# A decoder block with its residual turned by VectorE and small DMAs instead of TensorE, and its last outputs reordered

## The chip, the cores and the metric

One core of a Trainium2 chip runs the whole program. The metric is device time in microseconds (us) of one execution; the time before is 696.47 us, the median of three runs (696.46 to 696.84). The profile is one further execution of the same program, taken by the hardware profiler.

The engines are named as in the profile: PE is TensorE, PEld its weight load, DVE is VectorE, ACT is ScalarE, POOL is GpSimd, SP only issues DMAs. A "q" behind a name (SPq, ACTq) is that engine's queue issuing a DMA.

## The reference

One layer of a decoder on 512 positions with a model width of 1024, in float32. The parts in order:

```
h   = rms_norm(x, mix_norm)
z   = h @ w_in                       # u, v, c_q, c_kv, k_rope, gate_A, gate_B
y_a = gelu(u) * (tril(W_s) @ layer_norm(gelu(v)) + b)      # per chunk of 128 positions
y_b = latent attention of c_q, c_kv, k_rope                # 8 heads, causal
x   = x + (sigmoid(gate_A) * y_a + sigmoid(gate_B) * y_b) @ w_out
h   = rms_norm(x, ffn_norm)
up  = causal conv of width 3 of (h @ w_up)                 # 1024 -> 2 * 2816
x   = x + (silu(up[:2816]) * up[2816:]) @ w_down           # 2816 -> 1024
out = rms_norm(x, final_norm)
```

## The kernel before

Almost all work is matrix products. Each product of two float32 matrices is done as three TensorE products of operands split into a high part (rounded by an ACT copy to the type that PE takes) and a low part (the rest, a DVE subtraction): `mm3`, lines 79 to 82. A weight tile of 128 x 1024 is loaded into `wr` (three buffers), split into `wh` and `wl` (three buffers each, `wsplit`, lines 65 to 73), and used.

Activations stand transposed, with channels on partitions and the 512 positions along the row, in all parts but the last. The stages in time are: the small projections (`pS`, from 5 us on), v, the attention and gates, the product with w_out (`pout`), which leaves the residual `x1[j]`, eight tiles of 128 channels x 512 positions, then the up-projection (`pup`, 336 to 581 us) and the down-projection (`m`, 581 to 687 us).

The up-projection is a loop over n = 0 to 21 (line 653). Each n does two chunks of 24 matmuls (`up`, lines 621 to 628), the convolution (`conv`), the gate, and now and then `a_sides`, which prepares sums for the down-projection. The output must have positions on partitions, so the residual is turned on the way: for n = 4 to 11, `x1_turn` (lines 645 to 650) makes four PE transposes of 128 x 128 into a PSUM bank and an ACT copy of the bank back over the tile `x1t`. A turned row of 512 channels then lies in four pieces of 128 (512 bytes each).

The down-projection is computed in the manner of Strassen with seven products, in the order m1, m5, m6, m4, m3, m7, m2 (line 689). Each has 11 blocks of k in six steps (two blocks each, one in the last) for two output tiles (m = 0 and 1). The right-hand weights are sums that are formed by accumulating DMAs on POOL's queue into six tiles `R[g]` (`fill`, lines 604 to 608); the first fill and the one before m3 are plain loads on SP's queue. m2 reads its weights through `wr`. `a_split` (line 694) splits the left sides into tiles of tags h0 to h5, `w_split` (line 711) the weights two steps ahead. `post` (lines 751 to 775) adds the products to the residual; after the last product that touches an output tile, `done` adds it and has ACT square and sum it, and `finish` (lines 736 to 747) forms the inverse root on POOL, scales one half on DVE and the other on ACT, and stores both, one on SP's and one on ACT's queue. In m2 the last three steps are run for output tile 0 first and then for tile 1, so that tile 0 is finished while PE works on tile 1.

The order on each engine comes from a planner: it walks through the program with modelled costs and gives each engine the ready instruction that stands first in the program, so an instruction can run long before its place in the loop. A tile of a tag waits until the tile that held its buffer is no longer read.

The names that the change touches: `x1t` and `vA2` (lines 178 and 560, they share buffers by the tags d0 and d1), `x1_turn`, `fill`, `a_split`, `w_split`, `res`, `done`, `finish`, the loops of lines 653 and 796, and at the start the order of loads (lines 186 to 202) and the sum of squares `acc` (lines 211 to 222).

## Time and profile before

| what | value |
|---|---|
| median of three runs | 696.47 us (696.46 to 696.84) |
| the profiled execution | 697.01 us, of which the span from first to last instruction is 695.3 us |
| PE busy | 684.6 us (98% of the span), 3183 matmuls |
| DVE, ACT, POOL busy | 522.6, 353.9, 36.0 us |
| granted clock of PE, mean | 0.996 |
| HBM read, written | 76.02 MB, 2.10 MB |
| the last matmul begins | 686.15 us |

A row of the timeline has the start in us, the duration in us, engine, line, operation, the tile written, the tile read, and in brackets the idle time of that engine before it with what ended it. Matmuls overlap on PE, so the step from one start to the next says what one costs; the duration is longer than that.

### The profile page before, as it was taken

The numbers are of one execution on the slowest core, as the hardware profiler recorded it, in microseconds if no ns is written. First come the engines' busy times: TensorE is split into PE (matmuls) and PEld (weight loads), VectorE is DVE, ScalarE is ACT, GpSimd is POOL, SyncE is SP. The second block draws the span as 40 slices with busy tenths as digits, with TensorE's granted clock in tenths as the row PEclk, the third lists the DMA queues.
The fourth block names the chain that finished last, engine by engine and source line by source line (L and its number), as shares of the span: only waits on it lengthen the run. The fifth ranks groups of instructions, "written<-read, shape, count | busy, mean of one in ns | idle before, by whom it ended". The sixth has DMA issues, their size and how long they took to land.

```text
span 695.3 us, 8489 instructions
## 1 busy us (share of the span) xinstructions
PE 684.6 (98%) x3183; PEld 569.4 (82%) x3183; DVE 522.6 (75%) x859; ACT 353.9 (51%) x519; POOL 36.0 (5%) x42
## 2 busy tenths in 40 slices
PE   9999999999999999999999999999999999999994
PEld 6888888888888888888888888888888888888883
DVE  7966699877768678855577868778677789579884
ACT  6465556775765552343354344444344335565672
POOL 0000110000000000000100000000000002330201
PEclk9999999999999999999999999999999999999998
DMA  8424522131120112353542222223322236997824
GB/s 269 153 78 139 186 84 83 61 115 31 61 88 34 62 61 91 109 177 107 180 170 90 92 91 90 92 90 99 114 91 91 91 91 118 197 187 202 159 76 122
DMA packets 28026, 78.67 MB, mean 113 GB/s; under 512 B 3024, under 2 KB 7632, under 8 KB 27984
## 3 DMA queue, kind: packets, MB, share of 16 engines
q1 hardware_dynamic: 21408, 62.92, 27.4%
q0 software_dynamic: 3456, 11.54, 9.3%
q10 hardware_dynamic: 3120, 3.67, 1.7%
q8 instruction: 25, 0.41, 0.2%
q14 instruction: 17, 0.14, 0.1%
HBM read 76.02 MB, written 2.10 MB: 112 GB/s over the span
## 4 chain that ended last, share of the span: by engine, by line
PE 96%; DVE 1%; issue 1%; POOL 0%; ACT 0%; POOLq 0%
PE pup L80 12%; PE pup L82 12%; PE pup L81 11%; PE m L82 4%; PE m L81 4%; PE m L80 4%; PE pout L81 2%; PE pv L80 2%; PE pout L80 2%; PE pza L81 2%; PE pza L80 2%; PE pzb L80 2%; PE pzb L82 2%; PE pzu L81 2%; PE pzb L81 2%; PE pv L82 2%
## 5 line engine op out<-in xcount | busy, mean ns | idle before, releaser
L70 ACT CAST wh_u<-wr_u 128x1024 fp32r<-128x1024 f32 x44 | 46.3, 1051 | 84.4 <-issue 49.6
L71 DVE TENSOR_TENSOR wl_u<-wr_u,wh_u 128x1024 fp32r<-128x1024 f32 x44 | 53.9, 1224 | 9.9 <-ACT wh_u L70 9.6
L635 DVE TENSOR_TENSOR z<-pup,r 128x512 f32<-128x512 f32 x44 | 30.3, 690 | 40.3 <-PE pup L82 40.3
L82 PE MATMUL m<-wh_m,al_m 128*128 128x512 f32 x132 | 51.5, 390 | 0.6 <-DVE al_m L77 0.6
L80 PE MATMUL m<-wh_m,ah_m 128*128 128x512 f32 x132 | 51.4, 389 | 0.0
L81 PE MATMUL m<-wl_m,ah_m 128*128 128x512 f32 x132 | 51.4, 389 | 0.0
L70 ACT CAST wh_g<-wr_g 128x1024 fp32r<-128x1024 f32 x24 | 25.2, 1049 | 49.4 <-issue 30.6
L71 DVE TENSOR_TENSOR wl_m<-r,wh_m 128x1024 fp32r<-128x1024 f32 (+1 forms) x36 | 40.7, 1131 | 6.3 <-ACT wh_m L70 6.3
L70 ACT CAST wh_m<-r 128x1024 fp32r<-128x1024 f32 (+1 forms) x36 | 35.3, 980 | 19.6 <-PE m L82 19.1
L637 ACT ACTIVATE y<-z,part 128x512 f32<-128x512 f32 x44 | 35.7, 814 | 2.6 <-DVE z L635 2.4
L663 ACT ACTIVATE y<-y 128x512 f32<-128x512 f32 x22 | 13.9, 633 | 45.0 <-DVE y L641 45.0
L606 POOL DMA_DIRECT2D r<-in_w_d_dram x24 | 21.4, 890 | 287.0 <-DVE wl_m L71 270.7
L71 DVE TENSOR_TENSOR wl_g<-wr_g,wh_g 128x1024 fp32r<-128x1024 f32 x24 | 29.4, 1223 | 7.2 <-ACT wh_g L70 7.1
L641 DVE SCALAR_TENSOR_TENSOR y<-z,part,y 128x512 f32<-128x512 f32 x44 | 33.0, 751 | 1.4
L639 DVE SCALAR_TENSOR_TENSOR y<-z,part,y 128x512 f32<-128x512 f32 x44 | 32.8, 747 | 0.7 <-ACT y L637 0.7
L82 PEld LDWEIGHTS m<-wh_m,al_m 128*128 128x128 f32 x132 | 24.8, 188 | 6.1 <-DVE al_m L77 1.0
L81 PEld LDWEIGHTS m<-wl_m,ah_m 128*128 128x128 f32 x132 | 24.8, 188 | 5.2
L80 PEld LDWEIGHTS m<-wh_m,ah_m 128*128 128x128 f32 x132 | 24.8, 188 | 5.2
L81 PE MATMUL pout<-mL,wh_o 128*128 128x512 f32 x64 | 25.3, 395 | 0.0
L80 PE MATMUL pout<-mH,wh_o 128*128 128x512 f32 x64 | 25.0, 394 | 0.0
L82 PE MATMUL pout<-mH,wl_o 128*128 128x512 f32 x64 | 24.9, 389 | 0.0
L77 DVE TENSOR_TENSOR al_m<-aT,ah_m 128x1024 fp32r<-128x1024 f32 (+1 forms) x12 | 13.6, 1134 | 11.9 <-ACT ah_m L76 11.9
(565 smaller groups left out, 2004.0 us busy)
## 6 DMA issues: line engine op xcount, KB each, us to landing
wr_u<-in_w_u_dram SPq DMA_DIRECT2D x44, 512.0 KB, 3.3
wr_g<-in_w_g_dram SPq DMA_DIRECT2D x24, 512.0 KB, 3.4
r<-in_w_d_dram POOLq DMA_DIRECT2D x20, 512.0 KB, 7.2
r<-in_w_d_dram SPq DMA_DIRECT2D x10, 512.0 KB, 6.1
x<-in_xT_dram SPq DMA_DIRECT2D x16, 256.0 KB, 4.5
wr_v<-in_w_v_dram SPq DMA_DIRECT2D x8, 512.0 KB, 4.1
wr_o<-in_w_o_dram SPq DMA_DIRECT2D x8, 512.0 KB, 3.2
wr_m<-in_w_d_dram SPq DMA_DIRECT2D x5, 512.0 KB, 3.5
```

The lines of the kernel that those rows point to most:

```text
L70: A.copy(th[:, lo:hi], raw[:, lo:hi])
L71: V.tensor_tensor(out=tl[:, lo:hi], in0=raw[:, lo:hi], in1=th[:, lo:hi].bitcast(F32), op=ALU.subtract)
L77: V.tensor_tensor(out=tl, in0=src, in1=th.bitcast(F32), op=ALU.subtract)
L80: T.matmul(o, lhsT=wh, rhs=xh, start=start, stop=False)
L81: T.matmul(o, lhsT=wh, rhs=xl, start=False, stop=False)
L82: T.matmul(o, lhsT=wl, rhs=xh, start=False, stop=stop)
L606: G.dma_start(R[g], q[:, cols(g)], accum_op=ALU.add)
L635: V.tensor_tensor(out=z[:, 2:], in0=pz, in1=r2, op=ALU.mult)
L637: A.activation(out=y, in_=z[:, 2:], func=AF.Identity, scale=part[:, w + 2:w + 3], bias=part[:, PCB + f:PCB + f + 1])
L639: V.scalar_tensor_tensor(out=y, in0=z[:, 1:S + 1], scalar=part[:, w + 1:w + 2], in1=y, op0=ALU.mult, op1=ALU.add)
L641: V.scalar_tensor_tensor(out=y, in0=z[:, 0:S], scalar=part[:, w:w + 1], in1=y, op0=ALU.mult, op1=ALU.add)
L663: A.activation(out=yg, in_=yg, func=AF.Silu)
```

## The change

The residual is turned in two steps. `squares` has DVE transpose each `x1[j]` in blocks of 32 x 32 into a tile `xq` (eight instructions, n = 0 to 3). `x1_turn` then moves the blocks to their places in a new tile `xt` with DMAs on POOL's queue, each of 32 partitions x 4 x 32 elements (rows of 128 bytes): eight in each of n = 4 to 19, 128 in all. `xt` takes the buffer of `x1t`, which is now one tile, and `xq` the buffers of `R[0]` to `R[3]`. The first fill of `R` moves to n = 16 to 21 in the order 4, 5, 0, 1, 2, 3, and all fills go to POOL's queue.

In the down-projection the left side's last block of m2 gets tiles of its own and is split earlier (step 4 in place of 8); two of m2's six weight steps are split into buffers of `R`; `post` of a product is written three steps later in the program; m2's last four steps, not three, are run by output tile. `done` sums both halves' squares into the same cell and prepares all but one operation of the root; `finish` writes its result to a tile `o`, whose rows of 512 elements are stored as 2 KB each; tiles 0 and 2 share an `o` buffer, and so do tiles 1 and 3.

At the start, the first quarter of the first weights is loaded by ACT's queue ahead of everything else there, and the additions of squares come after the loop over j.

The diff, cut to what is spoken of:

```diff
+    ws0 = wp.tile([P, 1024], F32, tag="wr", name="wr_s0")
+    A.dma_start(ws0[:, :256], w_s[0, :, :256])
...
-    vA2 = [hp.tile([P, 2 * D], F32, tag=f"d{t}", name=f"vA{t}") for t in range(2)]
-    vA = [vA2[t // 2][:, (t % 2) * D:(t % 2 + 1) * D] for t in range(NT)]
+    vA4 = hp.tile([P, NT, D], F32, tag="d", name="vA")
+    vA = [vA4[:, t] for t in range(NT)]
...
-                    raws.append(wp.tile([P, 1024], F32, tag="wr", name="wr_s0"))
-                    for c in (slice(0, 256), slice(256, S)):
-                        SY.dma_start(raws[0][:, c], w_s[0, :, c])
+                    SY.dma_start(ws0[:, 256:S], w_s[0, :, 256:S])
...
-            sq = acc if j == 0 else st.tile([P, S], F32, tag="sq", name=f"sq{j}")
+            sq = acc if j == 0 else st.tile([P, S], F32, tag="sq", name=f"sq{j}", bufs=KC - 1)
+            sqx.append(sq)
...
-            if j:
-                V.tensor_tensor(out=acc, in0=acc, in1=sq, op=ALU.add)
+        for sq in sqx[1:]:
+            V.tensor_tensor(out=acc, in0=acc, in1=sq, op=ALU.add)
...
-        x1t = [hp.tile([P, NT, NT, P], F32, tag=f"d{t}", name=f"x1_{t}") for t in range(2)]
-        x1 = [x1t[j // NT][:, j % NT].rearrange("p t c -> p (t c)") for j in range(KC)]
+        x1t = hp.tile([P, KC, S], F32, tag="d", name="x1")
+        x1 = [x1t[:, j] for j in range(KC)]
...
-    R = [fp.tile([P, (hi - lo) * S], F32, name=f"r1_{lo}") for lo, hi in steps]
+    xq = [fp.tile([P, D], F32, tag=f"rr{q}", name=f"xq{q}") for q in range(KC // 2)]
+    R = [None] * NS
...
     def fill(q, g, add=True):
+        if R[g] is None:
+            R[g] = fp.tile([P, D], F32, tag=f"rr{g}", name=f"r1_{g}")
         if add:
-            G.dma_start(R[g], q[:, cols(g)], accum_op=ALU.add)
+            G.dma_start(R[g][:, :q[:, cols(g)].shape[1]], q[:, cols(g)], accum_op=ALU.add)
         else:
-            SY.dma_start(R[g], q[:, cols(g)])
+            G.dma_start(R[g][:, :q[:, cols(g)].shape[1]], q[:, cols(g)])
...
-    def x1_turn(t, hf):
-
-        pt = bank(f"pt{t}{hf}")
-        for q in range(NT):
-            T.transpose(pt[:, q * P:(q + 1) * P], x1t[hf][:, q, t, :], ident)
-        A.copy(x1t[hf][:, :, t, :], pt.rearrange("p (q c) -> p q c", q=NT))
+    def squares(j):
+        V.transpose(out=xq[j // 2][:, (j % 2) * S:(j % 2 + 1) * S], in_=x1[j])
+
+    xt = []
+
+    def x1_turn(j, rows):
+
+        if not xt:
+            xt.append(hp.tile([P, NT, D], F32, tag="d", name="xt"))
+        q = xq[j // 2][:, (j % 2) * S:(j % 2 + 1) * S].rearrange("p (t c f) -> p t c f", t=NT, c=NT)
+        for a in rows:
+            for c in range(NT):
+                G.dma_start(xt[0][32 * c:32 * c + 32, :, j * P + 32 * a:j * P + 32 * a + 32],
+                            q[32 * a:32 * a + 32, :, c])
...
-            if 4 <= n < 12:
-                x1_turn((n - 4) // 2, n % 2)
-            if 12 <= n < 12 + NS:
-                fill(B11, n - 12, False)
+            if n < 4:
+                squares(2 * n)
+                squares(2 * n + 1)
+            elif n < 20:
+                x1_turn((n - 4) // 2, (0, 1) if n % 2 == 0 else (2, 3))
+            if n >= NF - NS:
+                fill(B11, (n - NF + NS + 4) % NS, False)
...
-        ah = hp.tile([P, D], F32R, tag=f"h{b}", name=f"ah_{n}{lo}")
-        al = hp.tile([P, D], F32R, tag=f"h{3 + b}", name=f"al_{n}{lo}")
+        own = n == "m2" and b == 2
+        ah = hp.tile([P, D], F32R, tag=f"h{6 if own else b}", name=f"ah_{n}{lo}")
+        al = hp.tile([P, D], F32R, tag=f"h{7 if own else 3 + b}", name=f"al_{n}{lo}")
...
-        ws_[n, g] = wsplit(raw, f"{n}{g}", 0, w)
+        tiles = None
+        if n == "m2" and g in (2, 3):
+            tiles = tuple(fp.tile([P, D], F32R, tag=f"rr{2 * (g - 2) + k}", name=f"m2{g}{k}") for k in range(2))
+        ws_[n, g] = wsplit(raw, f"{n}{g}", 0, w, tiles)
...
-        return x1t[f][:, :, t, :]
-
-    def b3(t):
-        return t.rearrange("p (q c) -> p q c", q=NT)
+        return xt[0][:, t, f * S:(f + 1) * S]
...
+    def done(t, f, p_, op=ALU.add, last=False):
+        V.tensor_tensor(out=res(t, f), in0=res(t, f), in1=p_, op=op)
         j_ = dp.tile([P, S], F32, tag="j", name=f"j{t}{f}", bufs=2)
-        A.activation(out=b3(j_), in_=res(t, f), func=AF.Square, accum_out=ms[:, t, f:f + 1])
+        A.activation(out=j_, in_=res(t, f), func=AF.Square, accum_out=ms[:, t, 0:1])
+        if not last:
+            V.tensor_scalar(out=ms[:, t, 1:2], in0=ms[:, t, 0:1], scalar1=1.0 / D, scalar2=EPS,
+                            op0=ALU.mult, op1=ALU.add)
         if f:
-            V.tensor_tensor(out=res(t, f), in0=res(t, f), in1=b3(gfb[:, S:]), op=ALU.mult)
+            V.tensor_tensor(out=res(t, f), in0=res(t, f), in1=gfb[:, S:], op=ALU.mult)
...
-        V.tensor_scalar(out=ms[:, t, 2:3], in0=ms[:, t, 0:1], scalar1=ms[:, t, 1:2], scalar2=1.0 / D,
-                        op0=ALU.add, op1=ALU.mult)
-        V.tensor_scalar(out=ms[:, t, 2:3], in0=ms[:, t, 2:3], scalar1=EPS, scalar2=None, op0=ALU.add)
+        V.tensor_scalar(out=ms[:, t, 2:3], in0=ms[:, t, 0:1], scalar1=1.0 / D, scalar2=ms[:, t, 1:2],
+                        op0=ALU.mult, op1=ALU.add)
         G.tensor_tensor(out=ms[:, t, 3:4], in0=ms[:, t, 2:3], in1=mhalf[:, 0:1], op=ALU.pow)
         r_ = ms[:, t, 3:4]
-        V.scalar_tensor_tensor(out=res(t, 0), in0=res(t, 0), scalar=r_, in1=b3(gfb[:, :S]),
+        o = fp.tile([P, D], F32, tag=f"rr{(4, 5, 4, 5)[t]}", name=f"o{t}")
+        V.scalar_tensor_tensor(out=o[:, :S], in0=res(t, 0), scalar=r_, in1=gfb[:, :S],
                                op0=ALU.mult, op1=ALU.mult)
-        A.mul(res(t, 1), res(t, 1), r_)
-        SY.dma_start(out[t, :, :S], res(t, 0))
-        A.dma_start(out[t, :, S:], res(t, 1))
+        A.mul(o[:, S:], res(t, 1), r_)
+        SY.dma_start(out[t, :, :S], o[:, :S])
+        A.dma_start(out[t, :, S:], o[:, S:])
...
-            turn_.setdefault(b if i == 1 else NS * (i - 1) + (4, 6, 8)[b], []).append((n, b))
+            turn_.setdefault(b if i == 1 else NS * (i - 1) + (4, 6, 4 if n == "m2" else 8)[b], []).append((n, b))
...
+    late = {}
     for i, (n, g) in enumerate(seq):
         if i + 2 < len(seq):
             w_split(*seq[i + 2])
+        if i in late:
+            post(*late[i])
         for x in turn_.get(i, ()):
             a_split(*x)
         if g == 0:
             acc_ = [bank(f"{n}_{m}") for m in range(2)]
-        if n != order[-1] or g < NS - 3:
+        if n != order[-1] or g < NS - 4:
             steps_of(n, g, (0, 1))
             if g == NS - 1:
-                post(n, acc_)
+
+                late[i + 3] = (n, acc_)
 
     for m in range(2):
-        for g in range(NS - 3, NS):
+        for g in range(NS - 4, NS):
```

## Rows read from the trace of the kernel before

**Rows 1.** the page: busy time of each engine, with share of the span and instructions.
```profile
PE 684.6 (98%) x3183; PEld 569.4 (82%) x3183; DVE 522.6 (75%) x859; ACT 353.9 (51%) x519; POOL 36.0 (5%) x42
```

**Rows 2.** the page: the chain that ended last, share of the span by engine.
```profile
PE 96%; DVE 1%; issue 1%; POOL 0%; ACT 0%; POOLq 0%
```

**Rows 3.** windows: stretch, length, busy us of each engine (instructions), granted clock, DMA share, GB/s.
```profile
336.00:460.00 124.00, 124.00 (x563) 102.67 (x563) 88.38 (x134) 53.65 (x70) 1.84 (x1) 1.00 0.35 117
```

**Rows 4.** chain in order of time (start, us, what): first and last of eight.
```profile
392.08 0.44 PE pt L649 x4
...
471.64 0.44 PE pt L649 x4
```

**Rows 5.** PE in order of time: first products of two pup tiles, two chunks apart.
```profile
553.54 0.39 PE L80 MATMUL pup<-h0f,wh_u 128*128 128x512 f32 x1
...
564.42 0.39 PE L80 MATMUL pup<-h0f,wh_u 128*128 128x512 f32 x1
```

**Rows 6.** all engines in order of time, PE's wait in the last product.
```profile
680.97 0.39 PE L82 MATMUL m<-wh_m,al_m 128*128 128x512 f32 x1
...
681.94 0.50 PE L82 MATMUL m<-wh_m,al_m 128*128 128x512 f32 x1 [0.58 <-DVE al_m L77]
```

**Rows 7.** all engines in order of time, from the last outputs to the last store.
```profile
683.86 0.69 DVE L730 TENSOR_TENSOR x<-x,m 128x512 f32<-128x512 f32 x1 [1.37 <-PE m L82]
...
686.15 0.39 PE L82 MATMUL m<-wh_m,al_m 128*128 128x512 f32 x1
686.39 0.75 DVE L743 SCALAR_TENSOR_TENSOR x<-x,ms,gfb 128x512 f32<-128x512 f32 x1 [0.66 <-POOL ms L741]
687.06 0.68 DVE L730 TENSOR_TENSOR x<-x,m 128x512 f32<-128x512 f32 x1
...
688.53 0.21 DVE L738 TENSOR_SCALAR ms<-ms 128x1 f32<-128x1 f32 x1 [0.79 <-ACT j L732]
688.78 0.15 DVE L740 TENSOR_SCALAR ms<-ms 128x1 f32<-128x1 f32 x1
...
690.34 0.47 ACTq L747 DMA_DIRECT2D out_dram<-x  x1
```

**Rows 8.** DMA rate in 40 equal slices, 688 to 696 us, then 385 to 395.
```profile
GB/s 128 292 292 292 287 292 289 282 284 185 0 0 0 0 0 0 125 297 292 287 279 292 294 282 282 215 10 8 0 0 0 0 0 0 0 0 0 0 0 0
...
GB/s 360 442 393 311 33 0 0 0 0 0 0 0 66 0 0 0 0 0 0 0 0 164 164 49 377 377 442 426 99 0 0 0 0 0 0 0 0 0 0 0
```

**Rows 9.** the page: DMA issues: KB each, median us from issue to landing.
```profile
r<-in_w_d_dram POOLq DMA_DIRECT2D x20, 512.0 KB, 7.2
...
out_dram<-x ACTq DMA_DIRECT2D x4, 256.0 KB, 3.3
```

**Rows 10.** all engines in order of time, the first matmuls.
```profile
4.88 0.41 ACT L70 CAST wh_s<-wr_s 128x256 fp32r<-128x256 f32 x1 [0.49 <-DMA wr_s<-in_w_s_dram]
...
5.33 0.79 PE L80 MATMUL pS<-h0a,wh_s 128*128 128x512 f32 x1
...
5.92 0.63 PE L81 MATMUL pS<-h0a,wh_s 128*128 128x512 f32 x1
```

**Rows 11.** POOL in order of time: two DMA issues, one right behind the other.
```profile
614.12 0.88 POOL L606 DMA_DIRECT2D r<-in_w_d_dram  x1 [2.72 <-DVE wl_m L71]
615.41 0.88 POOL L606 DMA_DIRECT2D r<-in_w_d_dram  x1 [0.41 <-issue]
```

**Rows 12.** the page: DMA queues: packets, MB, share of 16 engines.
```profile
q0 software_dynamic: 3456, 11.54, 9.3%
q10 hardware_dynamic: 3120, 3.67, 1.7%
```

**Rows 13.** tile r: duration ns min/median/max, first and last start.
```profile
L606 POOL DMA_DIRECT2D r<-in_w_d_dram x24: 875/881/1063, 572.5 to 652.1; - x24
L608 SPq DMA_DIRECT2D r<-in_w_d_dram x12: 327/328/437, 339.7 to 636.1; - x12
```

**Rows 14.** ACT in order of time: the first read of r.
```profile
569.90 1.04 ACT L70 CAST wh_m<-r 128x1024 fp32r<-128x1024 f32 x1
```

More of the change, by code (lines that the diff above doesn't have):

```diff
@@ L177, in block_kernel @@
     ckL = mx.tile([P, S], F32R, name="ckL")
-    vA2 = [hp.tile([P, 2 * D], F32, tag=f"d{t}", name=f"vA{t}") for t in range(2)]
-    vA = [vA2[t // 2][:, (t % 2) * D:(t % 2 + 1) * D] for t in range(NT)]
+    vA4 = hp.tile([P, NT, D], F32, tag="d", name="vA")
+    vA = [vA4[:, t] for t in range(NT)]
     with tc.tile_pool(name="st", bufs=2) as st:
-        raws = []
+        raws = [ws0]
         xr = []
@@ L204, in block_kernel @@
         sw = [None] * 4
+        sqx = []
         for j in range(KC):
@@ L719, in res @@
     def res(t, f):
-        return x1t[f][:, :, t, :]
-    def b3(t):
-        return t.rearrange("p (q c) -> p q c", q=NT)
+        return xt[0][:, t, f * S:(f + 1) * S]
     def plus(t, f, t_):
-        V.tensor_tensor(out=res(t, f), in0=res(t, f), in1=b3(t_), op=ALU.add)
-    def done(t, f, p_, op=ALU.add):
-        V.tensor_tensor(out=res(t, f), in0=res(t, f), in1=b3(p_), op=op)
+        V.tensor_tensor(out=res(t, f), in0=res(t, f), in1=t_, op=ALU.add)
+    def done(t, f, p_, op=ALU.add, last=False):
+        V.tensor_tensor(out=res(t, f), in0=res(t, f), in1=p_, op=op)
@@ L769, in post @@
                 done(2 + m, 0, b[m])
-                done(2 + m, 1, b[m], ALU.subtract)
+                done(2 + m, 1, b[m], ALU.subtract, True)
                 finish(2 + m)
@@ L773, in post @@
                 with tc.high_priority():
-                    done(m, 0, b[m])
+                    done(m, 0, b[m], last=True)
                     finish(m)
```

## The prediction, made before the changed kernel was run

> **What bounds the kernel now.** I read the page's busy times first: PE is busy for 684.6 of 695.3 us, DVE for 522.6, POOL for 36.0 [rows 1]. The chain of waits then says that this work is also the path: 96% of the chain is PE [rows 2]. So time is won by taking matmul work from PE, by filling the few holes in PE's row, and by shortening what comes before the first and after the last matmul. In the stretch of the up-projection PE is busy for all 124.00 of 124 us, DVE for 88.38 and POOL for 1.84, and the DMA engines for 0.35 of the time [rows 3]; DVE has 36 us free there and POOL nearly everything. The only hole in PE's row of the down-projection is in the last product [rows 6], and after the last matmul, which begins at 686.15, come some 9 us of VectorE, ScalarE and store work [rows 7].
>
> **The sum is made against the profiled execution**, 697.01 us with a span of 695.3 (1.7 us lie outside the span). That execution is 0.54 us above the median of 696.47, so the result is carried over by taking the savings from the median.
>
> **PE transposes out.** The eight groups of four transposes begin at 392.08 to 471.64, one per n: (471.64 - 392.08) / 7 = 11.37 us per n with a group [rows 4]. Two chunks without one take 564.42 - 553.54 = 10.88 us (48 matmuls at 0.227) [rows 5]. A group thus costs PE 0.49 us and the eight 3.9 us. The chain books 0.44 for a group, which gives 3.5 as the lower end; 4.0 is the upper. PE has no holes here, so all of it is on the path. Their eight ACT copies go too; ACT is not on the path.
>
> **What takes their place.** Eight DVE transposes of 128 x 512: the trace has none. The nearest row is a 128x512 addition, 0.69 us [rows 7], so 5.5 us in all; at four times that, 22 us, they would still fit the 36 us that DVE has free before 460 [rows 3]. I cost them at nothing for PE, since weights are split two chunks (10.9 us) ahead; without that cover a transpose would cost its 0.7 us once or twice. Their place in the program is n = 0 to 3, but the planner runs what is ready: the first fill of `R`, written in n = 12, was issued at 339.7 [rows 13]. I expect the transposes in DVE's gaps before about 350.
>
> 128 DMAs on POOL's queue: each has 32 x 4 rows of 128 bytes, 128 pieces, as many as a fill has (3456 packets for 24 fills are 144 each, 128 and 16 that carry no data) [rows 12]. A fill costs POOL 0.88 us, 1.06 at most [rows 13], and two that stand right behind each other begin 1.29 us apart [rows 11]. I take 1.29: 128 x 1.29 = 165 us, from 350 to 515 us. Behind them POOL has the six first fills, 8 us to issue and 7.2 us to land [rows 9], so `R` is there at about 531; ACT first reads it at 569.90 [rows 14]. On POOL nothing else waits in that stretch. The bounds are 0.88 us (113 us in all) and a DMA that begins only when the one before has landed, at least the 3.3 us of a store (422 us); the limit is where the fills come late, (569.9 - 350 - 15) / 128 = 1.6 us. On the DMA engines, a packet of POOL's queue took 9.3% x 16 x 695.3 / 3456 = 0.30 us (4 KB, accumulating), one of ACT's queue 1.7% x 16 x 695.3 / 3120 = 0.06 us (1.2 KB on average) [rows 12]. 128 x 144 packets at 0.06 are 69 us of all 16 engines, which with the 0.35 in use fit 165 us. I take 0.06, since size decides more than the queue; at 0.30 they would be 346 us, and that belongs to the slower case below. The fills that move from SP's to POOL's queue cost SP nothing and POOL 0.9 us each. So: 3.9 won, 0 given back.
>
> **The hole in m2.** Two matmuls stand 681.94 - 680.97 = 0.97 us apart in place of 0.23, ended by DVE's `al_m` [rows 6], the block of the left side that now has its own tiles and an earlier place: 0.74 us won. Bounds 0 (another wait appears at the same place) and 0.8. The weights of m2 get two steps' worth of extra buffers, so the splits need not wait for PE; I see no stall that would be late next.
>
> **After the last matmul.** It ends at 686.54. For tile 1 the addition begins at 687.06, because DVE still has the scaling of tile 0 (686.39) in hand; for tile 0 it began as soon as PE was done [rows 7]. With four steps by tile instead of three, tile 0 is done 6 matmuls = 1.36 us earlier and that queueing of 0.5 us goes. Of the two small operations 0.25 us apart (688.53, 688.78) one remains: 0.25 won. Together 0.75; bounds 0.25 and 0.8. The scaled results go to `o` at the same cost.
>
> **The store.** The last two stores move 0.52 MB at about 292 GB/s in rows of 512 bytes, 1.8 us; loads with 4 KB rows reach 442 [rows 8], which would take 1.2. In rows of 2 KB I take 400 GB/s: 1.3 us, 0.5 won. Bounds 0 (the rate is that of writing) and 1.2 (issue and landing shorten too).
>
> **The start.** PE's first real matmul (5.33) waits for ACT's cast, which had waited 0.49 us for the first weights, and the second comes 0.59 us later [rows 10]; matmuls that wait for nothing stand 0.23 apart [rows 5]. With the load on ACT's queue at once, the cast no longer waits: 0.3 won. The warm-up matmuls stand in front of it on PE and keep it from being much more. Bounds 0 and 0.6. The additions of squares are moved behind the loop; they are the same seven, and their reader on PE stands behind the whole stage: 0.
>
> **Sum:** 3.9 + 0.74 + 0.75 + 0.5 + 0.3 = 6.2 us, 690.8 against the profiled execution and 690.3 against the median. The lower ends give 3.5 + 0 + 0.25 + 0 + 0 = 3.75, thus 692.7; the upper 7.4, thus 689.1.
>
> **The rivals.**
> *POOL or the small packets are too slow (slower).* If each small DMA holds POOL for over 1.6 us, the first fills land after ACT wants them and PE stops in front of m1, with nothing later to catch up. At 2.1 us (between 1.29 and 3.3): 350 + 128 x 2.1 + 15 = 634, then 2.3 us for cast and subtraction, so m1 starts at 636 and not at 580.75 less the 3.9 won: +59 us, about 750. At 0.30 us per packet the same happens through the DMA engines. Against it: POOL's 0.88 us doesn't wait for landing, since 1.29 us between two issues is far below 7.2 [rows 9, 11]. What would decide is whether 128 in a row keep that pace, which no row shows.
> The Trainium skill (DMA: Bandwidth & Descriptors, "Anatomy of one DMA") speaks against the change in this way: a DMA from POOL's queue has a fixed cost of about 2.0 us whatever its size. If that cost were paid one after the other, 128 x 2.0 = 256 us would put this rival's time near 737; if it overlaps, the forecast holds. The two issues 1.29 us apart bear out the overlap for two only.
>
> *The end is given back.* `post` of m7 is written three steps later (6 matmuls x 2 tiles per step, up to 6.8 us), and tile 0's result needs the `o` buffer that tile 2's store must have left (3.3 us to land) [rows 9]. In today's order that leaves some 2.7 us to spare; if the planner really moves tile 2's scaling by the whole 6.8 us, tile 0's scaling stands about 4 us in front of DVE's queue, and tile 1's addition behind it: +2.5 to 4 us on the forecast, about 693.5. For it: DVE works in order, and the last stage has it busy most of the time. Against it: the planner fills gaps, and with weights split earlier DVE has gaps before.
>
> *It changes nothing.* The PE time is real and PE's row has no holes, so this needs a loss that just cancels 4 to 6 us, such as DVE's transposes delaying the root of the second norm and then every chunk. Time 696.5.
>
> **How the numbers follow.** Forecast 0.67, the end given back 0.20, no change 0.05, too slow 0.08. A measurement of this kernel tells about 0.2% (1.4 us) from no change. Forecast and end given back are faster: 0.87; no change 0.05; slower 0.08. The forecast's own range is 689.1 to 692.7. To hold 8 in 10 it reaches to 694.3, through most of the second case, and down to 688.6; the too slow case is left out.
>
> **What would show each step.** Up-projection: no `pt` rows, chunks of 5.44 us throughout, PE busy for all of it. POOL: 128 DMA issues of about 0.9 us, 1.3 us apart, done near 515, and the first reading of `R` not ended by a DMA. Weight loads may land later than 3.3 us, harmless below 10. Last product: no matmul over 0.3 us behind its neighbour. End: addition within 0.05 us of the last matmul, one small DVE operation, store rate near 400 GB/s. The prediction is wrong if PE idles in front of m1, if DVE waits for a store ahead of writing `o`, or if POOL is still issuing small DMAs after 560.

## The result, and the profile after

The changed kernel takes 690.53 us (median of six runs, 690.25 to 692.8), the kernel before beside it 696.76 us (six, 696.46 to 697.14): a ratio of 0.9913, 95% interval 0.99 to 0.9927. The forecast was 690.3 us, its range 688.6 to 694.3. The profiled execution after is one of 690.42 us with a span of 688.6 us; all stretches below are of that one and of profiled executions of the other kernels.

The page of the kernel after, busy times and the chain:
```profile
PE 679.8 (99%) x3151; PEld 565.9 (82%) x3151; DVE 525.8 (76%) x867; ACT 350.0 (51%) x511; POOL 111.8 (16%) x182
...
PE 97%; issue 1%; DMA 0%; DVE 0%; ACT 0%; POOLq 0%; POOL 0%
```
PE has 32 instructions less than in [rows 1], the transposes, and is still the chain [rows 2]. POOL's 36.0 us became 111.8 us.

The window of the up-projection after, columns as in [rows 3]:
```profile
336.00:460.00 124.00, 124.00 (x552) 102.75 (x551) 95.16 (x146) 52.25 (x66) 75.27 (x135) 1.00 0.44 134
```
PE is as full as before, DVE has 6.8 us more and POOL 73 us more, and PE waits for neither.

The two new kinds of instruction, in the views of a line and of a tile (duration of one in ns, min/median/max, then first and last start in us; the landing is from issue to the data being there):
```profile
L653 DVE STREAM_TRANSPOSE xq<-x x8: 668/669/712, 339.3 to 346.3; 128x512 f32<-128x512 f32 x8
```
That is the line of the transposes; this is the tile that the DMAs write:
```profile
L664 POOL DMA_DIRECT2D xt<-xq x128: 551/551/617, 347.3 to 423.2; - x128
...
DMA to landing us min/median/max: 1.6/2.3/4.7
```
The 128 small DMAs begin (423.2 - 347.3) / 127 = 0.60 us apart, pauses included, half of the 1.29 that I took. Two of the six first fills were issued ahead of them, at 340.03; the other four come from 417.66 to 425.98, not behind 515:
```profile
408.92 8.69 POOL L664 DMA_DIRECT2D xt<-xq  x15 [0.15 <-issue]
417.66 0.58 POOL L615 DMA_DIRECT2D r<-in_w_d_dram  x1
418.24 1.72 POOL L664 DMA_DIRECT2D xt<-xq  x3
...
425.98 0.54 POOL L615 DMA_DIRECT2D r<-in_w_d_dram  x1 [1.00 <-DMA xt<-xq]
```

The end after, all engines in order of time; it answers to [rows 7]:
```profile
681.07 0.39 PE L82 MATMUL m<-wh_m,al_m 128*128 128x512 f32 x1
681.50 0.69 DVE L749 TENSOR_TENSOR xt<-xt,m 128x512 f32<-128x512 f32 x1 [1.66 <-PE m L82]
...
682.97 0.21 DVE L760 TENSOR_SCALAR ms<-ms 128x1 f32<-128x1 f32 x1 [0.79 <-ACT j L751]
...
683.85 0.75 DVE L765 SCALAR_TENSOR_TENSOR o<-xt,ms,gfb 128x512 f32<-128x512 f32 x1 [0.66 <-POOL ms L762]
684.60 0.37 ACTq L769 DMA_DIRECT2D out_dram<-o  x1
```
The addition begins 0.04 us after the last matmul's end (681.46), against 0.52 in [rows 7]. The last two stores, 684.6 to 688.6 us in 40 slices of 0.1 us (answers to [rows 8]; last columns of the issues: KB each, us to landing):
```profile
GB/s 0 0 0 0 0 0 0 0 143 348 369 451 348 410 348 369 369 471 369 369 369 369 144 0 0 0 0 0 0 0 0 0 0 0 0 0 0 0 0 0
...
out_dram<-o ACTq DMA_DIRECT2D x1, 256.0 KB, 2.8
```

Divided at four places that both kernels have, with a second profile of the kernel before (below, e10), the time went here (us):

| stretch | before | before again | after | won |
|---|---|---|---|---|
| start of the span to the first `pup` product | 336.05 | 335.40 | 335.74 | none shown |
| from there to the first product of m1 | 244.70 | 244.70 | 240.84 | 3.86 |
| to the start of the last product of m2 | 105.40 | 105.46 | 104.49 | 0.91 |
| to the issue of the last store | 4.19 | 4.18 | 3.53 | 0.66 |
| to the end of the span | 4.96 | 4.96 | 4.00 | 0.96 |

The last four rows of the kernel before repeat within 0.1 us; what is won in them adds up to 6.39 us, the medians differ by 6.23.

### The profile page after: what moved, and what is told of

It reads as the page before. It is cut to its first block, busy times and chain, and to the rows that moved or that the text cites. A ratio compares the mean times of both kernels' runs of the same rounds, so it can differ in the third digit from the quotient of the medians.

```text
span 688.6 us, 8556 instructions
## 1 busy us (share of the span) xinstructions
PE 679.8 (99%) x3151; PEld 565.9 (82%) x3151; DVE 525.8 (76%) x867; ACT 350.0 (51%) x511; POOL 111.8 (16%) x182
## 3 DMA queue, kind: packets, MB, share of 16 engines
q0 software_dynamic: 9152, 19.41, 13.6%
## 4 chain that ended last, share of the span: by engine, by line
PE 97%; issue 1%; DMA 0%; DVE 0%; ACT 0%; POOLq 0%; POOL 0%
PE pup L80 12%; PE pup L82 12%; PE pup L81 12%; PE m L82 5%; PE m L81 5%; PE m L80 5%; PE pout L81 2%; PE pv L80 2%; PE pout L80 2%; PE pza L81 2%; PE pza L80 2%; PE pzb L80 2%; PE pzb L82 2%; PE pzb L81 2%; PE pzu L81 2%; PE pv L82 2%
## 5 line engine op out<-in xcount | busy, mean ns | idle before, releaser
L664 POOL DMA_DIRECT2D xt<-xq x128 | 70.7, 553 | 9.0 <-DVE xq L653 3.8
L613 POOL DMA_DIRECT2D r<-in_w_d_dram x24 | 21.0, 873 | 188.9 <-DVE wl_m L71 167.5
L80 PE MATMUL m<-wh_m,ah_m 128*128 128x512 f32 x124 | 48.2, 389 | 0.0
L81 PE MATMUL m<-wl_m,ah_m 128*128 128x512 f32 x124 | 48.2, 389 | 0.0
L82 PE MATMUL m<-wh_m,al_m 128*128 128x512 f32 x124 | 48.2, 389 | 0.0
L615 POOL DMA_DIRECT2D r<-in_w_d_dram x12 | 6.9, 573 | 232.5 <-DVE acc L584 222.3
L80 PEld LDWEIGHTS m<-wh_m,ah_m 128*128 128x128 f32 x124 | 23.3, 188 | 4.9
L81 PEld LDWEIGHTS m<-wl_m,ah_m 128*128 128x128 f32 x124 | 23.3, 188 | 4.9
L82 PEld LDWEIGHTS m<-wh_m,al_m 128*128 128x128 f32 x124 | 23.3, 188 | 4.8
```

The costliest lines, as they stand in the source:

```text
L80: T.matmul(o, lhsT=wh, rhs=xh, start=start, stop=False)
L81: T.matmul(o, lhsT=wh, rhs=xl, start=False, stop=False)
L82: T.matmul(o, lhsT=wl, rhs=xh, start=False, stop=stop)
L613: G.dma_start(R[g][:, :q[:, cols(g)].shape[1]], q[:, cols(g)], accum_op=ALU.add)
L664: G.dma_start(xt[0][32 * c:32 * c + 32, :, j * P + 32 * a:j * P + 32 * a + 32], q[32 * a:32 * a + 32, :, c])
```

## The experiments

**e1: the transposes on PE again.** The edit, on the kernel after (the readers of the residual change only their views):
```
-            if n < 4:
-                squares(2 * n)
-                squares(2 * n + 1)
-            elif n < 20:
-                x1_turn((n - 4) // 2, (0, 1) if n % 2 == 0 else (2, 3))
+            if 4 <= n < 12:
+                x1_turn((n - 4) // 2, n % 2)
...
+            T.transpose(pt[:, q * P:(q + 1) * P], x1t[:, hf * NT + q, t * P:(t + 1) * P], ident)
+        A.copy(x1t[:, hf * NT:(hf + 1) * NT, t * P:(t + 1) * P], pt.rearrange("p (q c) -> p q c", q=NT))
```


> The kernel after, with one edit undone: the residual is turned by TensorE in place again (32 transposes of 128x128, ScalarE copies the banks back), no transposes on VectorE and no small DMAs on POOL; all other edits stay. Theory: PE sets the end, so its 32 transposes cost what they took in the kernel before: the first product of m1 starts at 576.6 + 3.9 = 580.4 us (580.0 to 580.6) and the median is 690.5 + 3.9 = 694.4 us (694.0 to 694.8). Rival: part of the gain came from ScalarE's and VectorE's load in the projection (the eight copies gone), and TensorE's transposes sat partly in its own small waits: then the first m1 product moves by less than 2.5 us and the median stays under 693.0 us.

Measured: 694.62 us median of five (694.27 to 696.12), 0.9971 of the kernel before (0.9957 to 0.9986). PE in order of time, the first product of m1:
```profile
580.92 0.39 PE L80 MATMUL m<-wh_m,a1h 128*128 128x512 f32 x1
```
That start is 0.3 us above the interval expected because this execution began late: its first `pup` product is at 336.22. Between the two lie 244.70 us, to the hundredth what the kernel before has. So the 3.86 us are the transposes' time on PE and nothing else, and with everything else of the change in place the kernel gives them back whole. The later stretches are those of the kernel after (104.50, 3.52 and 4.0 us), so the transposes are not what is won there.

**e2: stores in pieces of 512 bytes.**
```
-        V.scalar_tensor_tensor(out=o[:, :S], in0=res(t, 0), ...
+        ov = o.rearrange("p (q h c) -> p q h c", q=4, h=2)
...
+        V.scalar_tensor_tensor(out=ov[:, :, 0], in0=rv_[0], ...
...
-        A.dma_start(out[t, :, S:], o[:, S:])
+        A.dma_start(rv_[4], ov[:, :, 1])
```


> The kernel after, but the output tile is laid out with the two halves interleaved, so that each store takes four pieces of 512 bytes of a partition in place of one of 2 KB; bytes, queues and order are the same. Theory: the size of the rows made the last store shorter (4.96 to 4.00 us from its issue to the end of the span): here it is 4.9 us again (4.6 to 5.1), and the median is about 0.9 us up, 691.4 us. Rival: the last stores were shorter because fewer other transfers share the engines then, or because the issue is shorter: then it stays at 4.0 us (3.9 to 4.2) and the median within 0.3 us of 690.5.

Measured: 4.22 us from the last store's issue to the end, far below the theory's 4.6 to 5.1 and just above the rival's 3.9 to 4.2; but the median of four is 691.36 us (690.63 to 691.86), as the theory expected. The last stores, 684.6 to 688.6 us:
```profile
GB/s 0 0 0 0 0 0 0 0 0 164 302 276 297 282 297 287 297 292 292 287 287 297 282 272 292 287 287 154 16 0 0 0 0 0 0 0 0 0 0 0
...
out_dram<-o ACTq DMA_DIRECT2D x1, 256.0 KB, 3.2
```
The rate is that of the kernel before, some 290 GB/s [rows 8], and the data move for 1.9 us in place of 1.4. So the forecast's 0.5 us for the transfer is right, but of the 0.96 us won at the end the rows carry only 4.22 - 4.00 = 0.2 us in the span: the time after the last landing was shorter here (4.22 - 3.2 = 1.0 us against 4.00 - 2.8 = 1.2). e9 and e11 repeat it: 4.23 and 4.18. The medians say more, 0.83 us, and this execution was the fastest of its four: the spans of the others are 689.3, 689.8 and 690.0 against its 688.8. Where those lost their time no profile shows, and with four executions 0.8 us is not clear of the scatter (the ratio's interval, 0.9905 to 0.9934, overlaps that of the kernel after).

**e3 and e12: the first left operand ahead on VectorE.**
```
-                sw[pr] = wsplit(raws[pr], f"s{pr}", lo + a[0], lo + a[1], sw[pr])
+                with tc.issue_after(hi_.ins) if j == 0 else ExitStack():
+                    sw[pr] = wsplit(raws[pr], f"s{pr}", lo + a[0], lo + a[1], sw[pr])
```
(`hi_` is the second instruction of `h0a`.)

> The kernel after, with one order fixed by hand: on VectorE the two instructions that make the first left operand (h0a, 0.48 and 0.75 us) go ahead of the 0.43 us low part of the first weight columns. Theory: in the kernel after TensorE's first two products wait for h0a (5.45 and 6.15 us), so both come some 0.4 us earlier and the first block of the projection ends at 8.1 to 8.3 us in place of 8.55: median 690.1 us. Rival: the start is then followed by more products at the slow spacing of 0.43 us, as in the kernel before, or the weight's low part becomes the wait: the end of that block stays at 8.4 to 8.7 us and the median within 0.2 us of 690.5.

Measured: 690.21 us (four, 690.07 to 690.86); first `pup` product at 335.39. That looked like a gain, so it ran again:

> The kernel with h0a first on VectorE once more, in five rounds, as the version that might beat both kernels. Theory: the first block of the projection ends at 7.9 to 8.1 us in place of 8.4 to 8.6 us and some 0.3 us of that reach the end: median 690.0 to 690.4 us, the first product of the up-projection at 335.3 to 335.7 us. Rival: the later waits for weights in the first stage eat it, as the starts of the kernels with the old order scatter from 335.7 to 336.3 us anyway: 690.5 to 690.9 us.

Measured: 690.61 us (four, 690.39 to 690.88), 0.9907 of before (0.9891 to 0.9924); first `pup` product at 335.73, as in the kernel after. PE in order of time, the kernel after:
```profile
5.45 0.47 PE L80 MATMUL pS<-h0a,wh_s 128*128 128x512 f32 x1
6.15 0.50 PE L81 MATMUL pS<-h0a,wh_s 128*128 128x512 f32 x1 [0.22 <-DVE h0a L212]
6.49 0.39 PE L82 MATMUL pS<-h0a,wl_s 128*128 128x512 f32 x1
```
the first of the two executions with `h0a` ahead:
```profile
4.87 0.47 PE L80 MATMUL pS<-h0a,wh_s 128*128 128x512 f32 x1
5.57 0.51 PE L81 MATMUL pS<-h0a,wh_s 128*128 128x512 f32 x1 [0.22 <-DVE h0a L212]
5.91 0.40 PE L80 MATMUL pS<-h0a,wh_s 128*128 128x512 f32 x1
```
and the second:
```profile
4.96 0.77 PE L80 MATMUL pS<-h0a,wh_s 128*128 128x512 f32 x1
5.66 0.79 PE L81 MATMUL pS<-h0a,wh_s 128*128 128x512 f32 x1
6.25 0.63 PE L80 MATMUL pS<-h0a,wh_s 128*128 128x512 f32 x1
6.67 0.43 PE L82 MATMUL pS<-h0a,wl_s 128*128 128x512 f32 x1
```
Both begin 0.5 us earlier. The first then goes on at 0.23 us per product, the second has steps of 0.59 and 0.42 and ends the block at 8.56 us like the kernel after (8.55). The first profile of the kernel before has such slow steps too [rows 10], its second (e10) has not. Which of the two one gets isn't the program's doing here, so this is no version that beats both. The slow products take as long (0.79 and 0.63 us) as those behind a stop of PE in e5 (0.80 and 0.63), where the granted clock is 0.50 (593 to 597 us); here it is shown as 1.00 in either execution. So the lower clock fits their length, but the clock's own column speaks against it, and why the steps are slow stays open.

**e4: the last scaling and stores in two pieces.**
```
-        A.mul(o[:, S:], res(t, 1), r_)
-        SY.dma_start(out[t, :, :S], o[:, :S])
+        for a, b in ((0, S // 2), (S // 2, S)) if t == 1 else ((0, S),):
+            A.mul(o[:, S + a:S + b], xt[0][:, t, S + a:S + b], r_)
+            SY.dma_start(out[t, :, a:b], o[:, a:b])
...
```


> The kernel after, but the last row tile's final scaling and stores go in two column pieces on each of VectorE and ScalarE (four stores of 1 KB rows in place of two of 2 KB). Theory: the first piece's transfer is hidden by the second's scaling, so that half the bytes are left behind the last issue: the span's end comes 0.3 to 0.5 us earlier, median 690.0 to 690.2 us. Rival: a store is mostly fixed time, and the extra instructions cost 0.1 to 0.3 us on each engine: the last store is issued later by that and the time from its issue to the end shrinks by less, median 690.5 to 690.8 us.

Measured: 690.55 us (four, 690.35 to 691.1). VectorE's last instruction takes longer in two pieces:
```profile
684.17 0.88 DVE L766 SCALAR_TENSOR_TENSOR o<-xt,ms,gfb 128x256 f32<-128x256 f32 x2 [0.66 <-POOL ms L762]
```
0.88 us for two in place of 0.75, and the last issue comes at 685.10. From the last product's start (681.39) to the end of the span (688.9) are 7.5 us, as in the kernel after (681.07 to 688.6). The rival holds: what is hidden of the transfer is paid in instructions.

**e5: four times as many small DMAs.**
```
-                G.dma_start(xt[0][32 * c:32 * c + 32, :, j * P + 32 * a:j * P + 32 * a + 32],
-                            q[32 * a:32 * a + 32, :, c])
+                for t in range(NT):
+                    G.dma_start(xt[0][32 * c:32 * c + 32, t, j * P + 32 * a:j * P + 32 * a + 32],
+                                q[32 * a:32 * a + 32, t, c])
```


> The kernel after, but each small DMA of the turned residual moves one of its four row tiles alone: 512 DMAs of 32 pieces of 128 bytes in place of 128 of 128 pieces; pieces, bytes, queue and order are the same. In the kernel after the 128 keep POOL's queue 0.58 us apart, 76 us in all. Theory: what POOL pays is a price per DMA and hardly one per piece: 512 x 0.5 to 0.6 us = 256 to 307 us, so they end at 603 to 654 us, the first fills of R behind them land some 15 us later, and TensorE stops in front of m1 for 40 to 90 us: 730 to 785 us. Rival: the price is per piece (0.58 / 128 = 4.5 ns): 512 x 0.15 = 76 us again, done by 425 to 440 us, no stop, 690.5 us. Between the two (half fixed, half by piece: 0.36 us each, 186 us, done at 533) nothing stops either, but the issue times tell.

Measured: 723.98 us (one run; before beside it 697.19). The tile's view, duration of one in ns, then first and last start:
```profile
L665 POOL DMA_DIRECT2D xt<-xq x512: 496/498/567, 347.4 to 604.3; - x171
...
DMA to landing us min/median/max: 1.5/2.0/4.6
```
(604.3 - 347.4) / 511 = 0.50 us per DMA with 32 pieces, against 0.60 with 128: POOL pays per DMA, hardly per piece. The first fills come late, and PE stops twice for lack of weights, in front of m1 and behind its first step, 27.1 us in all; ScalarE's cast of the weights waits for the fill's DMA:
```profile
593.06 1.22 PE L80 MATMUL m<-wh_m,a1h 128*128 128x512 f32 x2 [16.17 <-ACT wh_m L70]
594.32 0.80 PE L81 MATMUL m<-wl_m,a1h 128*128 128x512 f32 x1
594.92 0.63 PE L82 MATMUL m<-wh_m,a1l 128*128 128x512 f32 x1
...
608.65 1.04 ACT L70 CAST wh_m<-r 128x1024 fp32r<-128x1024 f32 x1 [15.64 <-DMA r<-in_w_d_dram]
...
609.74 1.22 PE L80 MATMUL m<-wh_m,a1h 128*128 128x512 f32 x2 [10.93 <-ACT wh_m L70]
```
The loss is less than the 40 us expected at least, since the planner had put three of the first fills earlier (two at 340.19, ahead of the small DMAs, and one at 587.96, between them). Behind each stop, of 16.17 and 10.93 us without a product, PE runs slowly: from 594.92 to 598.33 its products stand 0.43 us apart in place of 0.23. The granted clock of these windows (the column of 0.61 and 0.53) lies between the two levels, near the lower, 1.2 GHz; columns as in [rows 3]:
```profile
593.00:600.00 7.00, 5.72 (x12) 3.64 (x12) 1.23 (x1) 0.01 (x1) 6.96 (x15) 0.61 0.06 8
600.00:609.00 9.00, 0.00 (x0) 0.00 (x0) 0.00 (x0) 0.35 (x1) 7.33 (x14) 0.61 0.34 113
609.00:616.00 7.00, 6.22 (x15) 4.45 (x16) 3.67 (x3) 3.11 (x4) 2.29 (x3) 0.53 0.99 217
```
This is the rival "POOL too slow" of the prediction, made real, and by the wait it named.

**e6, e7, e8: the edits of the last product, one at a time.** First the left block's own tiles and earlier place undone:
```
-        own = n == "m2" and b == 2
+        own = False
...
-            turn_.setdefault(b if i == 1 else NS * (i - 1) + (4, 6, 4 if n == "m2" else 8)[b], []).append((n, b))
+            turn_.setdefault(b if i == 1 else NS * (i - 1) + (4, 6, 8)[b], []).append((n, b))
```


> The kernel after, with one edit undone: the last block of the left side of m2 is split into the shared tiles again and at its old place in the order (step 8 and not 4 of the product before). The later post of each product and four steps by tile at the end stay. In the kernel before TensorE had a hole of 0.97 - 0.23 = 0.74 us in m2, ended by VectorE's al_m; in the kernel after it has none. Theory: this edit took it away: a hole of 0.4 to 0.9 us ended by al_m is back, and the time from the first product of m1 to the last product of m2 goes from 104.49 to 104.9 to 105.4 us. Rival: the later post had freed VectorE at that place already: no hole, 104.5 us.

Then the later post undone:
```
-                late[i + 3] = (n, acc_)
+                post(n, acc_)
```


> The kernel after, with one edit undone: each product's results are added up right behind its last step, not three steps of the next product later. The own tiles and the earlier place of the last left block of m2 stay. Theory: the own tiles alone keep VectorE's al_m early: no hole in m2, 104.5 us from the first product of m1 to the last of m2. Rival: without the later post VectorE's additions stand ahead of the splits of weights at the start of each product, and TensorE waits 0.2 to 1 us in one or more of them: 104.7 to 106 us.

Then three steps by tile in place of four:
```
-        if n != order[-1] or g < NS - 4:
+        if n != order[-1] or g < NS - 3:
...
-        for g in range(NS - 4, NS):
+        for g in range(NS - 3, NS):
```


> The kernel after, with three steps by tile at the end of m2 in place of four. Theory: the first tile is then done 6 matmuls (1.36 us) later, VectorE still has its scaling in hand when TensorE ends, and the last tile's addition begins 0.5 us after TensorE's end and not 0.04: from the start of the last matmul to the last store's issue 4.0 us in place of 3.53, median +0.5 us. Rival: with one small VectorE operation less in the chain the first tile's scaling is done in time anyway: 3.5 to 3.6 us, no change.

Measured: 690.84, 690.85 and 691.0 us (one run each); from the first product of m1 to the last of m2 104.50, 104.51 and 104.49 us, no hole in any; from the last product to the last store's issue 3.52, 3.53 and 3.52 us. In all three the only difference to the kernel after is the start (336.18, 336.30 and 336.34 against 335.74). So my theory fell in e6 and e8, and held in e7. VectorE in order of time with three steps by tile:
```profile
681.03 0.75 DVE L765 SCALAR_TENSOR_TENSOR o<-xt,ms,gfb 128x512 f32<-128x512 f32 x1 [0.65 <-POOL ms L762]
682.09 0.69 DVE L749 TENSOR_TENSOR xt<-xt,m 128x512 f32<-128x512 f32 x1 [0.30 <-PE m L82]
```
The scaling of the first tile is over 0.3 us before the last tile's addition is wanted. By these rows the reason is the hole: in the kernel before 12 products follow the first tile's last one (683.43 to 686.15), here 15, since there the planner's order has three of the second tile's products ahead of it, next to the hole. Three products, 0.68 us, cover the 0.48 us of queueing in [rows 7]; the small VectorE operation less, some 0.2 us, would not by itself. Without the hole three steps are enough here.

**e9 and e11: what does take the hole away.** Both edits of e6 and e7 undone together, and 512-byte pieces for the stores in passing (edits as above):

> The kernel after with both edits of the two runs before undone together: the last left block of m2 in the shared tiles at its old place, and each product's results added up at once. Beside that, in another stretch, the stores take pieces of 512 bytes once more. With either edit alone undone TensorE had no hole. Theory for the hole: the two cover for each other, so with both undone VectorE's al_m is late again: 0.3 to 0.9 us between two products of m2, 104.7 to 105.4 us from the first product of m1 to the last of m2. Rival: neither does it; the two additional pairs of tiles for the weights of m2, or the order that the planner finds since TensorE's transposes are gone, do: no hole, 104.5 us. For the stores: with rows as the whole cause of the 0.96 us, 4.9 us from the last store's issue to the end; if it is 4.2 to 4.4 us, as in the first run with such pieces, rows are a quarter to a half of it.

Measured: 690.72 us; m1 to m2 104.56 us, no hole; the stores 4.23 us. The theory fell again, and against one of the rival's two causes, the order without TensorE's transposes, stands e1, which has them back and no hole. So a third edit was undone beside these two:
```
-        if n == "m2" and g in (2, 3):
+        if False:
             tiles = tuple(fp.tile([P, D], F32R, tag=f"rr{2 * (g - 2) + k}", name=f"m2{g}{k}") for k in range(2))
```
(For the 2 KB distance of the stores' pieces, `R[4]` and `R[5]` become halves of one tile there.)

> The kernel after with a third edit undone beside the own tiles and the later post: the weights of m2's third and fourth step no longer have tiles of their own. In another stretch, the stores take pieces of 512 bytes that lie 2 KB apart in a partition, as in the kernel before (in the two runs with such pieces so far they lay 1 KB apart). For the hole: if the additional weight tiles kept it away, a hole of 0.3 to 0.9 us ended by al_m or wl_m is back and the time from m1's first to m2's last product is 104.8 to 105.4 us; if the order that the planner finds with TensorE's transposes and the first fills moved is the cause, 104.5 us still. For the stores: if the distance of the pieces made the stragglers of the kernel before, 4.9 us from the last store's issue to the end; if not, 4.2 us.

Measured: 692.6 us (one run); m1 to m2 106.18 us, 1.69 more and beyond the 105.4 expected; the stores 4.18 us. The waits between 660 and 680 us (engine line waited for: us in total, times, longest):
```profile
ACT wh_m L70 <- PE m L82: 2.9, 3, 1.1
...
PE m L81 <- DVE wl_m L71: 1.0, 2, 0.9
```
In the same view the kernel after has no wait of PE's, and that wait of ScalarE's only once:
```profile
ACT wh_m L70 <- PE m L82: 0.9, 1, 0.9
```
And with four steps by tile the queueing at the end is back too: the scaling at 682.86, the addition 0.3 us late at 683.53, 3.81 us from the last product to the last issue. What the extra tiles do stands in VectorE's rows. With them, in e9, four of the six low parts of m2's weights have begun by 666.87, and the low part of the last left block follows at 672.57:
```profile
672.57 0.95 DVE L77 TENSOR_TENSOR al_m<-aT,ah_m 128x768 fp32r<-128x768 f32 x1
```
Without them, in e11, two have begun by then (664.54 and 666.55), the others stand among the last additions and scalings, and `al_m` comes 5 us later; PE's first stop is ended by one of those weights:
```profile
674.10 1.22 DVE L71 TENSOR_TENSOR wl_m<-wr_m,wh_m 128x1024 fp32r<-128x1024 f32 x1
675.37 0.50 PE L81 MATMUL m<-wl_m,ah_m 128*128 128x512 f32 x1 [0.85 <-DVE wl_m L71]
677.56 0.95 DVE L77 TENSOR_TENSOR al_m<-aT,ah_m 128x768 fp32r<-128x768 f32 x1
```
So the old buffers make VectorE's row late: in e11 as in the kernel before, where `al_m` begins at 680.93, 100.2 us behind m1's first product (100.9 in e11, 95.9 in e9). With the four extra tiles the left block's own tiles and the later post change nothing that PE's row shows. But e11 is not the hole of the kernel before: its stops are ended by `wl_m`, not by `al_m`, and cost more. It has four steps by tile on three weight buffers, where the kernel before has three steps: the last cast (677.54) waits 1.07 us for PE to be done with a tile, which the last cast of the kernel before (680.89) does not. The old tiles with three steps were not run. The three were not undone one against the other in all ways: that the extra tiles are enough is e9, that they are needed is shown only with the other two undone. The distance of the pieces is not what lengthened the stores of the kernel before.

**e10: the kernel before again.**

> The kernel before, unchanged, for a second profile of its start and its end. Six executions with the start of the kernel after had their first product of the up-projection between 335.72 and 336.34 us, mean 336.1; the one profile of the kernel before has 336.05. Theory: the start won nothing, and 336.05 is an ordinary value: here 335.7 to 336.4 us. Rival: the start won some 0.3 us on average: 336.4 us or later. For the end: if 4.96 us from the last store's issue to the end of the span is what this kernel does, 4.8 to 5.1 us here; if it was one long end by chance, 4.2 to 4.6 us.

Measured: 696.46 us. Start at 335.40, earlier than the kernel after has it and below what theory and rival expected; the hole is there again, to 0.01 us:
```profile
4.74 0.84 PE L80 MATMUL pS<-h0a,wh_s 128*128 128x512 f32 x1
5.42 0.39 PE L81 MATMUL pS<-h0a,wh_s 128*128 128x512 f32 x1
5.66 0.40 PE L80 MATMUL pS<-h0a,wh_s 128*128 128x512 f32 x1
...
335.40 0.39 PE L80 MATMUL pup<-h0f,wh_u 128*128 128x512 f32 x1
...
681.32 0.50 PE L82 MATMUL m<-wh_m,al_m 128*128 128x512 f32 x1 [0.58 <-DVE al_m L77]
```
and the end, 4.96 us. The last stores, 689.7 to 694.7 us in 40 slices:
```profile
GB/s 0 0 0 0 0 0 0 29 246 311 279 295 287 283 283 287 291 299 283 283 291 336 152 4 16 8 0 0 0 0 0 0 0 0 0 0 0 0 0 0
...
q14 instruction: 1, 0.01, 0.4%
...
out_dram<-x ACTq DMA_DIRECT2D x1, 256.0 KB, 3.8
```
Ten profiles with the start code of the kernel after have their first `pup` product between 335.72 and 336.34 us, mean 336.0; two of the kernel before 336.05 and 335.40. The start won nothing that can be told. The end is no chance. Its tail of 4 to 16 GB/s would fit one of the 16 DMA engines still at work (290 / 16 = 18 GB/s), and in this window the instruction queue has one packet of 0.4% x 16 x 5.0 = 0.32 us, which e2, e9 and e11 do not have there. The first profile of the kernel before has the same packet between 693 and 694 us. That this packet gets in the way of the last store fits, but nothing was run that moves it alone.

## Why the prediction was right, and where it was not

**PE transposes out (3.9): right.** 3.86 us, within 0.03 in the nine other profiles that have the edit and no stop, and e1 gives them back alone.

**What takes their place (0): right, with the pace mis-sized.** DVE's transposes took 0.67 us (forecast 0.69) and fell in 339 to 347. POOL's 128 DMAs took 76 us, not 165: 1.29 came from two accumulating fills [rows 11], and accumulating is what costs: 0.87 us and a pause of 0.4, as in the kernel after too (609.80, 611.09), while two plain fills right behind each other take 1.09 us together (e5, 604.75) and a small DMA 0.55. Even the lower bound of 0.88 was above the 0.60 measured. The packets were fewer as well: POOL's queue has 9152 in all; less 36 fills of 144 [rows 12] that is 31 for each small DMA and not the 144 that I took. The cover was therefore wider than thought: the last of the first fills was issued at 426 and not near 523, and ACT first reads one at 565.73, waiting for no DMA. e5 shows where the cover ends, by the forecast's own limit: at 512 DMAs, 257 us of POOL, it costs 33 us. The Trainium skill (DMA: Bandwidth & Descriptors, "Anatomy of one DMA") gives about 2.0 us fixed for each DMA of this queue and says that most of it is completion latency. The trace agrees: some 2 us is the landing (2.3 and 2.0 us) and not the pace (0.60 and 0.50), so it overlaps.

**The hole (0.74): right in size, wrong in its cause.** 0.91 us were won: the hole's 0.74, the slow step behind it (0.33 in place of 0.23), and less than 0.1 in the rest. I put it to the left block's own tiles, because the waiting product names `al_m` [rows 6]. e6 has the old tiles and no hole, e9 as well, and only e11, without the weight tiles too, has PE waiting again. Those tiles the forecast had only as an aside ("so the splits need not wait for PE"). They are enough (e9 against e11: `al_m` at 672.57 or 677.56); that the same lateness made the hole of the kernel before is argued from the place of `al_m` in VectorE's row, since e11's stops are others.

**After the last matmul (0.75): 0.66.** The queueing of 0.48 us went, but not through the four steps by tile (e8): it went with the hole, and came back in e11 with four steps in place. The rest, some 0.2, fits the one small operation less, which no run undid alone.

**The store (0.5): mis-sized, 0.96.** The transfer is 0.5 us shorter by the rows of 2 KB (e2), as forecast. In the profiled spans this is 0.2 us, by three profiles with 512-byte pieces (4.22, 4.23, 4.18 against 4.00), while e2's median, 0.83 us up, would give rows nearly all of it. By the profiles 0.74 us belong to something that the kernel before does and none of these does. The landing shows 0.6 of it (3.8 to 3.2 us). It is not the distance of the pieces (e11); the instruction packet is the only other thing that the trace shows, and this stays open.

**The start (0.3): wrong, none shown.** ACT's cast does begin 0.83 us earlier (4.05 against 4.88 in [rows 10]), but then DVE makes `wl_s` ahead of `h0a`, and PE's first product waits for `h0a` until 5.45. The wait and the slow second step that the term was made from are no trait of the kernel before: in e10 the cast begins at 4.28, with no wait before it, PE at 4.74, and the first block of the projection is done 0.6 us or more earlier than in any of the ten profiles with the new start (the next block begins at 7.96 there, at 8.60 to 8.88 in the ten, at 9.03 in the first profile of before). The 0.31 us between the first two profiles was scatter (e10).

**The sum** of 6.2 us met 6.23 (6.39 by the profiles). For the transposes, nearly two thirds of it, this is the mechanism; for the rest the nearness is luck: the store's 0.46 too little made up for the start's 0.3 too much, and the hole's size came from an edit that did not cure it. Of the rivals, "the end is given back" did not come: with `post` three steps later the scalings of tiles 2 and 3 stood at 673.57 and 675.71 in DVE's row, and no write to `o` waited for a store. The 2.7 us to spare that it was argued with stand in no row; after, tile 2's stores, issued at 674.3 to 674.4, landed within 2.8 us, some 1.9 us before tile 0's scaling at 679.09.

## What to carry to other kernels

Here one engine was full, and what left it was won in full (3.86 of 3.9 us), so work could go to a far clumsier place, 128 DMAs, because its end lay well ahead of the first reader; work out that limit and count the issues, not the bytes. A wait names what came last, not what made it late: the hole named `al_m`, and with buffers for the weights alone it did not come back (e9). A term below the scatter of its stretch needs two profiles of the kernel before: the first products of the up-projection lay 0.65 us apart in two executions of one program, and the 0.3 us at the start could not be told from that.

## What the runs showed of the hardware

A plain DMA held POOL for 0.55 us and an accumulating one for 0.87; 512 of 32 pieces took 0.50 us each and 128 of 128 pieces 0.55, so, as an estimate, 0.05 us for 96 pieces, some 0.5 ns per piece. DVE's turn of 128x512 fp32 in blocks of 32 took 0.67 us, as long as an addition of that size. The last two stores together moved some 290 GB/s in pieces of 512 bytes and some 380 in rows of 2 KB. From the last landing to the end of the span 1.0 to 1.2 us passed, and of a landing 0.4 us earlier 0.2 were left in the span (e2 against the kernel after). Products behind a stop of 16 us stepped 0.43 us at a granted clock of 0.50, in place of 0.23 at 1.00 (e5, 593 to 597 us).
